# x is turned without its norm, the tokens' factors follow at the evacuations, and the value columns are the first products

## The chip, the cores and the metric

One NeuronCore of a Trainium2 chip runs the whole program. The metric is device microseconds of one execution, the median of the runs shown. Before: 913.82 us, median of three runs (913.37 to 915.99).

## The reference, cut to what matters

The program computes two transformer blocks over 256 tokens of width 1024. The change touches the beginning of the first block alone:

```python
def rmsnorm(x, g):
    xf = x.astype(jnp.float32)
    y = xf * lax.rsqrt(jnp.mean(xf * xf, axis=-1, keepdims=True) + EPS)
    return (y * g.astype(jnp.float32)).astype(x.dtype)

hn = rmsnorm(h, norm_mix_g[l])
proj = hn @ w_in[l]
fq, fk, fv, ff, gq, gf, gi, gg = jnp.split(proj, split_idx, axis=-1)
```

The factor rsqrt(...) is one number per token, g one number per column of x. A factor per token can be applied to x or to each row of the product x g @ w_in; the result is the same but for rounding. fq, fk, fv (512 columns each) and ff (8 columns, forget gates) go to an attention; gq, gf, gi, gg (512 each) to a gated recurrence in chunks (q, forget gate, input, output gate).

## The kernel before

Each product is made in three passes of TensorE: both operands are split into a high part (fp32r) and a low part (the rest), and `mm3` (L205) adds high x high, low x high and high x low into PSUM. `split_to` (L321) splits the tokens' side: ScalarE writes the high part (L328 with a factor per partition), VectorE the low one (L329). The tokens lie transposed in `XT` = (`xh`, `xl`): 8 blocks of 128 columns of x on the partitions, 256 tokens along the row.

The weights come in granules of 1 MB (`Granule`, L31), loaded on SP's queue by `feed` (L117) into three raw buffers and split in two halves each (`split_next`, L129): ScalarE casts the high part (L142), VectorE subtracts (L143). At most six split halves exist; `pump` (L153) splits one more half after each unit of products. A unit is 24 products over one half granule: `a_units` (L210) puts weight columns on the partitions of the result and 256 tokens along the row; `b_units` (L244) and `fv_units` (L887) put 128 tokens on the partitions and 512 (or 2 x 260) columns along the row. Their results take both buffers of the PSUM tags `mm` (and, for fv, both of `tp`).

`emit` (L181) runs through the list of units: the unit's products, what the units before have put off (`then`, L196), one `pump`, the evacuation from PSUM, and the pieces hung on that index in the table at L1040 (the recurrence's `levels`, `forget`, the attention's S, T, V, tables, memory rows). TensorE's order is this one, written out. Inside `start` (L628) every engine's own instructions keep their written order; elsewhere a planner orders all engines but TensorE, by readiness and program order, and may put later instructions into gaps.

`start` loads the gain, x in two token halves and the first granule; TensorE runs twelve products on the identity meanwhile. Squares (ScalarE and VectorE), the power -0.5 on GpSimd (L297), the scaling of x (L651, L653), 16 transposes (L669) and 8 splits follow, with the first granule's split in four pieces, whose low parts GpSimd subtracts (L149). The units then come in the order gf, gq, gg, fv with ff, fq and fk, gi. gf is evacuated by a sigmoid, gq and gg by SiLU on ScalarE straight from PSUM (L753, L767), fq by ScalarE (L272), fk by VectorE (L270), fv and ff half by half on both (L909 to L911). `forget` (L920) transposes ff and takes the logarithm of its sigmoid; the recurrence's levels are eight small f32 products each (L792, L812) with VectorE's decays (L801, L802) and masked copies.

## Time and profile before

| | us |
|---|---|
| median of 3 runs | 913.82 |
| the profiled execution | 914.16 |
| its span, first to last instruction | 912.3 |
| TensorE busy | 898.0 (98%) |
| VectorE busy | 588.4 (64%) |
| ScalarE busy | 488.8 (54%) |
| GpSimd busy | 130.0 (14%) |

The profile comes from one execution. TensorE's busy time is that of overlapping products, whose ends are modelled, so the distance between starts tells more than the busy share. A wait is put down to the instruction or transfer that came last.

### The profile page before, as it was taken

What the parts mean: (1) busy time and instruction counts of PE and PEld (TensorE: products, weight loads), DVE (VectorE), ACT (ScalarE), POOL (GpSimd) and SP (SyncE); (2) the same over time, 40 slices, a digit from 0 to 9 for tenths busy, and PEclk for the clock granted to TensorE, in tenths of its full rate; (3) what the DMA queues carried; (4) which work ended last, traced back from release to release, by engine and by line L of the source; (5) the groups of instructions that cost most, each with busy time, mean ns of one, the idle gap of its engine ahead of it and who ended that gap; (6) DMA issues with size and microseconds to landing.
All of it is one profiled execution on the core that took longest, in us unless ns stands there. A gap on an engine that the chain in (4) does not pass through costs nothing.

```text
span 912.3 us, 15217 instructions
## 1 busy us (share of the span) xinstructions
PE 898.0 (98%) x6213; PEld 823.9 (90%) x6213; DVE 588.4 (64%) x858; ACT 488.8 (54%) x743; POOL 130.0 (14%) x141
## 2 busy tenths in 40 slices
PE   8999999999999999999999999999999999999997
PEld 7999898898899999999898899999998789999995
DVE  5778775755575444555776455776756777766664
ACT  6745753555455444444654545667443676555552
POOL 3102220000002111111104000221211201101101
PEclk9999999999999999999999999999999999999999
DMA  8776544543555555555374555434555455555531
GB/s 271 256 253 186 185 155 164 198 153 114 167 193 192 195 190 193 189 185 185 131 250 135 183 179 185 139 131 133 200 185 185 161 185 183 188 201 193 166 135 47
DMA packets 117972, 162.39 MB, mean 178 GB/s; under 512 B 3647, under 2 KB 90509, under 8 KB 117901
## 3 DMA queue, kind: packets, MB, share of 16 engines
q1 hardware_dynamic: 117901, 161.41, 53.4%
q8 instruction: 49, 0.80, 0.3%
q14 instruction: 22, 0.18, 0.1%
HBM read 160.34 MB, written 1.06 MB: 177 GB/s over the span
## 4 chain that ended last, share of the span: by engine, by line
PE 90%; DVE 4%; ACT 2%; DMA 2%; POOL 1%; issue 1%; SPq 0%; DVEq 0%; POOLq 0%; ACTq 0%
PE mm L206 19%; PE mm L207 19%; PE mm L208 19%; PE s L208 8%; PE s L206 8%; PE s L207 8%; DMA w<-in_w_in_dram 2%; PE s L792 1%; POOL sm L297 1%; DVE wl L143 1%; PE tp L1068 1%; PE s L1060 1%; PE tp L337 1%; ACT wh L142 1%; PE s L1212 1%
## 5 line engine op out<-in xcount | busy, mean ns | idle before, releaser
L143 DVE TENSOR_TENSOR wl<-w,wh 128x1024 fp32r<-128x1024 f32 (+1 forms) x283 | 355.4, 1261 | 182.4 <-ACT wh L142 180.8
L142 ACT CAST wh<-w 128x1024 fp32r<-128x1024 f32 (+1 forms) x284 | 296.1, 1048 | 306.0 <-PE mm L207 190.2
L206 PE MATMUL mm<-xh,wh 128*128 128x256 f32 x1120 | 317.8, 284 | 0.0
L207 PE MATMUL mm<-xl,wh 128*128 128x256 f32 x1120 | 313.9, 280 | 0.3
L208 PE MATMUL mm<-xh,wl 128*128 128x256 f32 x1120 | 313.3, 280 | 0.0
L206 PEld LDWEIGHTS mm<-xh,wh 128*128 128x128 f32 x1120 | 211.3, 189 | 3.9 <-issue 2.3
L207 PEld LDWEIGHTS mm<-xl,wh 128*128 128x128 f32 x1120 | 211.2, 189 | 2.0 <-DVE xl L329 0.7
L208 PEld LDWEIGHTS mm<-xh,wl 128*128 128x128 f32 x1120 | 211.3, 189 | 0.0
L206 PE MATMUL s<-wh,mh 128*128 128x512 f32 x176 | 69.8, 396 | 0.0
L207 PE MATMUL s<-wl,mh 128*128 128x512 f32 x176 | 69.0, 392 | 0.0
L208 PE MATMUL s<-wh,ml 128*128 128x512 f32 x168 | 66.1, 393 | 0.0
L297 POOL TENSOR_TENSOR sm<-sm,half 128x1 f32<-128x1 f32 (+2 forms) x24 | 20.3, 847 | 234.2 <-DVE sm L310 221.7
L1103 POOL TENSOR_TENSOR r<-r 128x512 f32<-128x512 f32 x16 | 25.3, 1583 | 148.6 <-ACT r L1101 148.6
L206 PE MATMUL mm<-eh,wh 128*128 128x256 f32 x160 | 45.7, 286 | 0.0
L207 PE MATMUL mm<-el,wh 128*128 128x256 f32 x160 | 44.8, 280 | 0.0
L208 PE MATMUL mm<-eh,wl 128*128 128x256 f32 x160 | 44.7, 280 | 0.0
L208 PE MATMUL s<-wh,mh 128*128 128x512 f32 x112 | 44.1, 393 | 0.0
L1362 POOL TENSOR_TENSOR r<-r 128x512 f32<-128x512 f32 x11 | 21.4, 1946 | 148.0 <-DVE r L1350 124.2
L206 PE MATMUL s<-wh,ml 128*128 128x512 f32 x104 | 40.9, 394 | 0.0
L207 PE MATMUL s<-wl,ml 128*128 128x512 f32 x104 | 40.7, 392 | 0.0
L207 PEld LDWEIGHTS s<-wl,mh 128*128 128x128 f32 x176 | 33.1, 188 | 6.9
L206 PEld LDWEIGHTS s<-wh,mh 128*128 128x128 f32 x176 | 33.1, 188 | 6.7
(273 smaller groups left out, 1377.7 us busy)
## 6 DMA issues: line engine op xcount, KB each, us to landing
w<-in_w_in_dram SPq DMA_DIRECT2D x39, 1024.0 KB
w<-in_w_dram SPq DMA_DIRECT2D x32, 1024.0 KB
w<-in_w_up_dram SPq DMA_DIRECT2D x22, 1024.0 KB
w<-in_w_down_dram SPq DMA_DIRECT2D x11, 1024.0 KB
w<-in_w_xkv_dram SPq DMA_DIRECT2D x8, 1024.0 KB
w<-in_w_out_dram SPq DMA_DIRECT2D x8, 1024.0 KB
w<-in_w_xq_dram SPq DMA_DIRECT2D x4, 1024.0 KB
w<-in_w_xo_dram SPq DMA_DIRECT2D x4, 1024.0 KB
```

The costliest lines, as they stand in the source:

```text
L142: S.copy(hi, src)
L143: low.tensor_tensor(lo, src, hi.bitcast(F32), op=ALU.subtract)
L206: PE.matmul(o, lh, rh, start=first, stop=False)
L207: PE.matmul(o, lh, rl, start=False, stop=False)
L208: PE.matmul(o, ll, rh, start=False, stop=last)
L297: G.tensor_tensor(r[:, :n], v[:, :n], half.to_broadcast([P, n]), op=ALU.pow)
L337: PE.transpose(o[:, k * P:(k + 1) * P], xn[:, kk * P:(kk + 1) * P], ident)
L792: PE.matmul(o, k_[:, x], q2, start=True, stop=True)
L1060: PE.matmul(s[:, t, :], xq[:, j, t * P:(t + 1) * P], xkT[:, j, :], start=(c == 0), stop=(c == 1))
L1068: PE.matmul(o[:, c * T:(c + 1) * T], xv[:, m, cs], pt[:, m, :], start=(m == 0), stop=(m == 1))
L1103: G.tensor_tensor(tt, ra, ra, op=ALU.mult)
L1362: G.tensor_tensor(yv, yg, yv, op=ALU.mult)
```

## The change

- The first granule is now the upper half (512 rows) of the 520 columns of fv and ff, loaded in three transfers between the two halves of x; the gain vector is loaded on ScalarE's queue. Eight products on the identity stand in for twelve.
- x is transposed as it is, one token half after the other; the splits are of 128x128 with the gain as factor. After each half come the twelve products of the first half granule with these tokens (`fv_part`). All low pieces of the first granule are subtracted by VectorE.
- The squares, sums and powers come behind that; the tokens' factors go to `rt` (a column per token half) and, by one product of ones with a diagonal, to `rB` (the 256 factors in a row on every partition; `row_factors`).
- Evacuations multiply by the tokens' factor: `ev_token` and `ev_gf` on VectorE with `rB`, SiLU and sigmoid in place afterwards on ScalarE; gg, fv, ff and gi with `rt` on ScalarE or VectorE.
- The units come in the order fv (the other three), gf, gq, gg, fq and fk, gi; the table of pieces is adapted: `forget` at index 4, the levels at 12 to 20.

```diff
...
@@ -142,11 +138,11 @@
             S.copy(hi, src)
             low.tensor_tensor(lo, src, hi.bitcast(F32), op=ALU.subtract)
         else:
-            k = g.nk // 2
+            k = shape[1] // 2
             for p in (np.s_[:, 0:k, :], np.s_[:, k:, :]):
                 def piece(p=p):
                     S.copy(hi[p], src[p])
-                    G.tensor_tensor(lo[p], src[p], hi[p].bitcast(F32), op=ALU.subtract)
+                    V.tensor_tensor(lo[p], src[p], hi[p].bitcast(F32), op=ALU.subtract)
                 pieces.append(piece)
         feed()
 
@@ -202,10 +198,13 @@
         later.append(go)
 
 
-    def mm3(o, lh, ll, rh, rl, first, last):
+    def mm3(o, lh, ll, rh, rl, first, last, rl_last=False):
         PE.matmul(o, lh, rh, start=first, stop=False)
-        PE.matmul(o, lh, rl, start=False, stop=False)
-        PE.matmul(o, ll, rh, start=False, stop=last)
+        if rl_last:
+            PE.matmul(o, ll, rh, start=False, stop=False)
+        PE.matmul(o, lh, rl, start=False, stop=last and rl_last)
+        if not rl_last:
+            PE.matmul(o, ll, rh, start=False, stop=last)
 
     def a_units(src, xt, evac, nk=8):
 
@@ -624,13 +623,24 @@
     hgrn_g = vt[:, 100:101]
     subln_g = vt[:, 101:102]
     w_in = a["w_in"][0]
+    rt = const.tile([P, 2], F32, name="rt")
+    rB = R[3][:, 1792:2048]
+    rB2 = rB.unsqueeze(1).to_broadcast([P, 2, T])
 
     def start():
         xin = a["x"][0].rearrange("(t p) d -> p t d", p=P)
         grow = R[5][0:8, 0:P]
-        nc.sync.dma_start(grow, a["norm_mix_g"][0].rearrange("(k p) -> k p", p=P))
-        for t in range(2):
-            nc.sync.dma_start(h[:, t, :], xin[:, t, :])
+        nc.scalar.dma_start(grow, a["norm_mix_g"][0].rearrange("(k p) -> k p", p=P))
+
+        w0 = stream[0]
+        w0.raw = wraw.tile([P, w0.nk, w0.ncol], F32, tag="w", name=nm("w"))
+        src = w0.src.rearrange("(k p) c -> p k c", p=P)
+        nc.sync.dma_start(h[:, 0, :], xin[:, 0, :])
+        for k in range(2):
+            nc.sync.dma_start(w0.raw[:, k, :], src[:, k, :])
+        nc.sync.dma_start(h[:, 1, :], xin[:, 1, :])
+        nc.sync.dma_start(w0.raw[:, 2:4, :], src[:, 2:4, :])
+        at_dma[0] = 1
         feed()
         V.memset(half, -0.5)
         V.memset(one, 1.0)
@@ -638,35 +648,34 @@
         g = const.tile([P, 8], F32, name="g8")
 
         o = mm_t()[:, 0:P]
-        for _ in range(12):
+        for _ in range(8):
             PE.matmul(o, ident, ident, start=True, stop=True)
         go = mm_t()[:, 0:8]
         PE.transpose(go, grow, ident[0:8, 0:8])
-        o = [x.rearrange("p (k t) -> p k t", k=2) for x in (s_t(), s_t(), s_t(), s_t(), tp_t(), tp_t())]
-        o = [o[k][:, 0, :] for k in range(6)] + [o[k][:, 1, :] for k in (2, 3)]
-
-        def scale(t, n, r):
-            x = xn_half(t)[:, HALVES[n]]
-            if n > t:
-                S.mul(x, h[:, t, HALVES[n]], r[:, 0:1])
-            else:
-                V.tensor_scalar(x, h[:, t, HALVES[n]], r[:, 0:1], None, op0=ALU.mult)
-
+        V.tensor_copy(g, go)
+        pieces = []
+        for _ in range(2):
+            split_next(pieces)
+
+        def turn(t):
+
+            o = [s_t(), s_t()]
+            for k in range(8):
+                PE.transpose(o[k // 4][:, k % 4 * P:(k % 4 + 1) * P], h[:, t, k * P:(k + 1) * P], ident)
+            for k in range(8):
+                split_to(XT, np.s_[:, k, t * P:(t + 1) * P], o[k // 4][:, k % 4 * P:(k % 4 + 1) * P], g[:, k:k + 1])
+                if k % 2 and len(pieces) > 2 * (1 - t):
+                    pieces.pop(0)()
+
+        for t in range(2):
+            turn(t)
+            fv_part(0, t)
+        release()
         ss = [sm_t(), sm_t()]
-        for n in range(2):
-            square(h[:, 0, HALVES[n]], ss[0][:, n:n + 1], (S, V)[n])
-        r0 = rstd_row(ss[0])
-        scale(0, 0, r0)
-        for n in range(2):
-            square(h[:, 1, HALVES[n]], ss[1][:, n:n + 1], (S, V)[n])
-        scale(0, 1, r0)
-        r1 = rstd_row(ss[1])
-        for n in range(2):
-            scale(1, n, r1)
-        V.tensor_copy(g, go)
         for t in range(2):
-            for k in range(8):
-                PE.transpose(o[k][:, t * P:(t + 1) * P], xn_half(t)[:, k * P:(k + 1) * P], ident)
+            for n in range(2):
+                square(h[:, t, HALVES[n]], ss[t][:, n:n + 1], (S, V)[n])
+            V.tensor_copy(rt[:, t:t + 1], rstd_row(ss[t])[:, 0:1])
 
         st1 = ppool.tile([P, 768], F32, tag="P", name="st1")
         st2 = ppool.tile([P, 768], F32, tag="P", name="st2")
@@ -678,16 +687,6 @@
         nc.sync.dma_start(st1[101:102, :P], a["subln_g_2"])
         nc.sync.dma_start(st2[0:88, :P], a["conv_w_2"][0, 0:2].rearrange("l (c p) -> (l c) p", p=P))
         lvlf = ppool.tile([P, 768], F32, tag="PT", name="lvlf")
-        pieces = []
-        for _ in range(2):
-            split_next(pieces)
-        for p in pieces[0:2]:
-            p()
-        for k in range(8):
-            split_to(XT, np.s_[:, k, :], o[k], g[:, k:k + 1])
-            if k in (5, 7):
-                pieces[k // 2]()
-
         def vectors():
             pv = tp_t()
             PE.transpose(pv[:, 0:102], st1[0:102, :P], ident[0:102, 0:102])
...
+        def row_factors():
+
+            ones, diag = R[4][:, 0:P], R[4][:, P:3 * P]
+            G.memset(ones, 1.0)
+            for t in range(2):
+                V.tensor_scalar(diag[:, t * P:(t + 1) * P], ident, rt[:, t:t + 1], None, op0=ALU.mult)
+            o = s_t()[:, 0:T]
+            PE.matmul(o, ones, diag, start=True, stop=True)
+            V.tensor_copy(rB, o)
+
         def load_tables():
             nc.sync.dma_start(lvlf[:, 0:512], a["c_lvl"])
             nc.sync.dma_start(fbias, a["fox_f_bias"].rearrange("o h -> h o"))
@@ -729,12 +738,13 @@
             V.tensor_scalar(nlam, nlam, -0.2, None, op0=ALU.add)
 
         start.vectors, start.tables, start.difference = vectors, tables, difference
-        start.load_tables, start.load_later = load_tables, load_later
+        start.load_tables, start.load_later, start.row_factors = load_tables, load_later, row_factors
 
     def start_in_order():
         with tc.manual_schedule():
             start()
 
+    stream.append(Granule(w_in[0:512, 1024:1544], 4, 520, False))
     do(start_in_order)
 
 
@@ -750,7 +760,9 @@
     def ev_gf(g):
         def ev(i, o):
             s = slice(g * 512, (g + 1) * 512)
-            S.activation(f_[:, s], o, AF.Sigmoid)
+            V.tensor_tensor(f_[:, s].rearrange("p (b t) -> p b t", b=2), o.rearrange("p (b t) -> p b t", b=2), rB2,
+                            op=ALU.mult)
+            S.activation(f_[:, s], f_[:, s], AF.Sigmoid)
 
             def rest():
                 for b in range(2):
@@ -762,9 +774,16 @@
             then(rest)
         return ev
 
-    def ev_silu(dst):
+    def ev_token(dst, scale=None, silu=False):
+
         def ev(i, o):
-            S.activation(dst, o, AF.Silu)
+            d, o = (x.rearrange("p (b t) -> p b t", b=2) for x in (dst, o))
+            if scale is None:
+                V.tensor_tensor(d, o, rB2, op=ALU.mult)
+            else:
+                V.scalar_tensor_tensor(d, o, scale, rB2, op0=ALU.mult, op1=ALU.mult)
+            if silu:
+                S.activation(dst, dst, AF.Silu)
         return ev
 
 
@@ -884,34 +903,37 @@
 
     ff = []
 
-    def fv_units():
-        gs_ = [Granule(w_in[kq * 512:(kq + 1) * 512, 1024:1544], 4, 520, False) for kq in range(2)]
-        st = {}
-
-        def unit(i):
-            if i == 0:
-                st["o"] = [(mm_t(), tp_t()) for _ in range(2)]
-            w = part(gs_[i // 2], i % 2)
+    fv_g = [stream[0], Granule(w_in[512:D, 1024:1544], 4, 520, False)]
+    fv_o = []
+
+    def fv_part(i, t):
+        if len(fv_o) == t:
+            fv_o.append((mm_t(), tp_t()))
+        w = part(fv_g[i // 2], i % 2)
+        tok = slice(t * P, (t + 1) * P)
+        for k in range(2):
+            for c in range(2):
+                cs = slice(c * 260, (c + 1) * 260)
+
+                mm3(fv_o[t][c][:, 0:260], r32(xh[:, 2 * i + k, tok]), r32(xl[:, 2 * i + k, tok]),
+                    w[0][:, k, cs], w[1][:, k, cs], i == 0 and k == 0, i == 3 and k == 1, True)
+
+    def fv_unit(i):
+        for t in range(2):
+            fv_part(i, t)
+        release()
+
+        def ev():
             for t in range(2):
-                tok = slice(t * P, (t + 1) * P)
-                for k in range(2):
-                    for c in range(2):
-                        cs = slice(c * 260, (c + 1) * 260)
-                        mm3(st["o"][t][c][:, 0:260], r32(xh[:, 2 * i + k, tok]), r32(xl[:, 2 * i + k, tok]),
-                            w[0][:, k, cs], w[1][:, k, cs], i == 0 and k == 0, i == 3 and k == 1)
-            release()
-
-            def ev():
-                for t in range(2):
-                    copy = V.tensor_copy if t else S.copy
-                    o = st["o"][t]
-                    ff.append(sm_t())
-                    copy(fv[:, t, 0:260], o[0][:, 0:260])
-                    copy(ff[t], o[1][:, 252:260])
-                    copy(fv[:, t, 260:512], o[1][:, 0:252])
-            return ev if i == 3 else None
-
-        return [(lambda i=i: unit(i), gs_[i // 2] if i % 2 == 0 else None) for i in range(4)]
+                o, r = fv_o[t], rt[:, t:t + 1]
+                ff.append(sm_t())
+                for dst, src in ((fv[:, t, 0:260], o[0][:, 0:260]), (ff[t], o[1][:, 252:260]),
+                                 (fv[:, t, 260:512], o[1][:, 0:252])):
+                    if t:
+                        V.tensor_scalar(dst, src, r, None, op0=ALU.mult)
+                    else:
+                        S.mul(dst, src, r)
+        return ev if i == 3 else None
 
 
     fox_bias = [x.rearrange("p (e c) -> p e c", e=2) for x in
@@ -1025,27 +1047,30 @@
 
 
     m_load, m_s0, m_s1, m_t0, m_t1 = mem_rows("mem", "norm_mem_g", R[5], s_t)
-    u_ = []
+    u_ = [(lambda i=i: fv_unit(i), fv_g[1] if i == 2 else None) for i in range(1, 4)]
     for g in range(2):
         u_ += a_units(cols(w_in, 2056, g), XT, ev_gf(g))
     for g in range(2):
-        u_ += a_units(cols(w_in, 1544, g), XT, ev_silu(q_[:, g * 512:(g + 1) * 512]))
-    u_ += b_units(w_in[:, 3080:3592], XT, lambda t, o: ev_silu(gs[:, t * 512:(t + 1) * 512])(0, o))
-    u_ += fv_units()
+        u_ += a_units(cols(w_in, 1544, g), XT, ev_token(q_[:, g * 512:(g + 1) * 512], silu=True))
+    u_ += b_units(w_in[:, 3080:3592], XT, lambda t, o: S.activation(gs[:, t * 512:(t + 1) * 512], o, AF.Silu,
+                                                                    scale=rt[:, t:t + 1]))
     for g in range(2):
-        u_ += a_units(cols(w_in, 0, g), XT, ev_to(R[2][:, g * 512:(g + 1) * 512], 0.125))
-        u_ += a_units(cols(w_in, 512, g), XT, ev_to(R[2][:, 1024 + g * 512:1024 + (g + 1) * 512]))
-    u_ += rows(w_in, 2568, 1, gi) + grid(xkw, 0, 4, R[5], None, ME)
+        u_ += a_units(cols(w_in, 0, g), XT, ev_token(R[2][:, g * 512:(g + 1) * 512], 0.125))
+        u_ += a_units(cols(w_in, 512, g), XT, ev_token(R[2][:, 1024 + g * 512:1024 + (g + 1) * 512]))
+    u_ += b_units(w_in[:, 2568:3080], XT, lambda t, o: (V.tensor_scalar(gi[:, 1, :], o, rt[:, 1:2], None, op0=ALU.mult)
+                                                        if t else S.mul(gi[:, 0, :], o, rt[:, 0:1])))
+    u_ += grid(xkw, 0, 4, R[5], None, ME)
     fox = Heads(fox_scores, fox_turn, fox_pv)
-    run(u_, {
-        1: [lambda: start.vectors()], 2: [lambda: start.load_tables()], 6: [lambda: start.tables()],
-        7: [lambda: start.load_later()], 9: [levels[0]], 11: [levels[1]],
-        12: [m_load, levels[2], lambda: start.difference()], 13: [levels[3]], 14: [levels[4]], 15: [forget],
-        16: [levels[5], m_s0], 17: [levels[6]], 18: [levels[7], m_s1, load_bias(0)], 19: [levels[8]],
-        20: [load_bias(1, 2, 3)], 21: [fox.S(0)], 23: [fox.T(0), fox.S(1)], 25: [fox.V(0), m_t0],
-        26: [fox.S(2), m_t1], 27: [fox.T(1)], 28: [fox.S(3), h_out(0)], 29: [fox.V(1), h_out(1)],
+    at = {
+        2: [lambda: start.load_tables()], 3: [lambda: start.row_factors()], 4: [lambda: start.vectors()], 5: [forget],
+        8: [load_bias(0)], 7: [lambda: start.tables()], 11: [lambda: start.load_later()],
+        13: [levels[0], m_load], 14: [levels[1]], 15: [levels[2], lambda: start.difference()], 16: [levels[3], m_s0],
+        17: [levels[4]], 18: [levels[5], m_s1], 19: [levels[6]], 20: [levels[7]], 21: [levels[8], fox.S(0)],
+        22: [load_bias(1, 2, 3)], 23: [fox.T(0)], 24: [fox.S(1)], 25: [fox.V(0), m_t0],
+        26: [fox.T(1), m_t1], 27: [fox.S(2)], 28: [fox.V(1), h_out(0)], 29: [fox.S(3), h_out(1)],
         30: [fox.T(2)], 31: [h_turn(0)], 32: [fox.V(2), fox.T(3)], 33: [h_turn(1)], 34: [fox.V(3)],
-    })
+    }
+    run(u_, {i - 1: x for i, x in at.items()})
     fill_xv = rows(xkw, D, 2, xv, ME)
     out_stage(a["w_out"][0], MT, Tail, lambda: [gain("norm_x_g")], fill_xv[0:4])
 
```

## Rows read from the trace of the kernel before

**Rows 1.** The profile's page: busy time by engine; the chain that ended last.
```profile
PE 898.0 (98%) x6213; PEld 823.9 (90%) x6213; DVE 588.4 (64%) x858; ACT 488.8 (54%) x743; POOL 130.0 (14%) x141
...
PE 90%; DVE 4%; ACT 2%; DMA 2%; POOL 1%; issue 1%; SPq 0%; DVEq 0%; POOLq 0%; ACTq 0%
```
**Rows 2.** Windows: stretch, length, busy time per engine, granted clock, DMA share, GB/s.
```profile
0.00:5.00 5.00, 3.65 (x17) 3.66 (x18) 0.22 (x3) 1.41 (x2) 0.69 (x6) 1.00 0.49 169
5.00:10.00 5.00, 3.84 (x22) 2.93 (x21) 3.42 (x9) 3.07 (x7) 2.39 (x3) 1.00 1.10 320
10.00:15.00 5.00, 4.11 (x27) 3.50 (x28) 3.96 (x10) 4.27 (x11) 3.96 (x5) 1.00 1.09 347
...
14.83:35.00 20.17, 20.17 (x174) 20.17 (x173) 16.40 (x27) 17.61 (x19) 5.07 (x6) 1.00 0.77 252
35.00:146.00 111.00, 109.80 (x854) 101.20 (x854) 80.94 (x147) 58.12 (x102) 16.83 (x22) 1.00 0.60 197
```
**Rows 3.** Timeline of TensorE, the start: start us, us, engine, line, operation.
```profile
1.34 5.49 PE L642 MATMUL mm<-ident 128*128 128x128 f32 x24 [1.34 <-POOL ident masks.py:199]
...
7.12 0.66 PE L669 MATMUL s<-ident,r 128*128 128x128 f32 x4
...
11.26 0.38 PE L206 MATMUL mm<-xh,wh 128*128 128x256 f32 x1
...
15.23 0.28 PE L206 MATMUL mm<-xh,wh 128*128 128x256 f32 x1
...
18.07 0.25 PE L693 MATMUL tp<-ident,st 102*128 102x102 f32 x1
```
**Rows 4.** Timeline of the other engines and SP's queue, the start.
```profile
1.18 0.83 SPq L633 DMA_DIRECT2D h<-in_x_dram  x2
...
4.87 0.63 ACT L304 ACTIVATE junk<-h 128x512 bf16<-128x512 f32 x1 [2.87 <-DMA h<-in_x_dram]
...
5.98 0.56 POOL L297 TENSOR_TENSOR sm<-sm,half 128x1 f32<-128x1 f32 x1 [4.69 <-DVE sm L310]
...
10.73 1.57 ACT L328 ACTIVATE xh<-s,g 128x256 fp32r<-128x256 f32 x4 [1.55 <-DVE g L666]
...
11.24 1.66 DVE L329 SCALAR_TENSOR_TENSOR xl<-s,g,xh 128x256 fp32r<-128x256 f32 x4 [0.60 <-ACT xh L328]
...
11.63 0.95 POOL L710 MEMSET r<- 128x1024 f32 x1
...
13.62 2.55 POOL L149 TENSOR_TENSOR wl<-w,wh 128x512 fp32r<-128x512 f32 x2 [1.04 <-ACT wh L148]
```
**Rows 5.** Groups by line and shape: count | busy us, mean ns | idle before.
```profile
L143 DVE TENSOR_TENSOR wl<-w,wh 128x1024 fp32r<-128x1024 f32 x36 | 45.6, 1277 | 10.8 <-ACT wh L142 10.8
...
L357 DVE CUSTOM_DVE_ANT_0 P<-s,r 128x128 f32<-128x128 f32 x8 | 2.3, 288 | 5.2 <-issue 3.6 <-DMA r<-negF 1.6
...
L142 ACT CAST wh<-w 128x1024 fp32r<-128x1024 f32 x36 | 37.1, 1052 | 47.7 <-PE mm L207 23.5 <-PE tp L208 8.2 <-issue 7.2
...
L909 ACT COPY r<-mm 128x260 f32<-128x260 f32 x1 | 0.4, 376 | 1.8 <-PE mm L208 1.8
...
L812 PE MATMUL s<-r,r 128*128 128x128 f32 x16 | 1.9, 275 | 0.0
```
**Rows 6.** Timeline around the two stalls behind the start: TensorE, ScalarE, VectorE.
```profile
36.35 0.39 PE L208 MATMUL mm<-wh,xl 128*128 128x512 f32 x1
36.88 0.50 PE L206 MATMUL mm<-wh,xh 128*128 128x512 f32 x1
...
67.14 0.27 PE L924 MATMUL s<-ident,sm 128*8 128x128 f32 x1
67.90 0.27 PE L924 MATMUL s<-ident,sm 128*8 128x128 f32 x1 [0.49 <-DVE sm L910]
...
36.24 0.59 ACT L767 ACTIVATE r<-mm 128x512 f32<-128x512 f32 x1
...
66.22 1.21 DVE L143 TENSOR_TENSOR wl<-w,wh 128x1024 fp32r<-128x1024 f32 x1
```

More of the change, by code (lines that the diff above doesn't have):

```diff
@@ L121, in feed @@
             src = g.src.rearrange("(k p) c -> p k c", p=P)
-            if at_dma[0]:
-                nc.sync.dma_start(g.raw, src)
-            else:
-                for c in (slice(0, P), slice(P, 2 * P)):
-                    nc.sync.dma_start(g.raw[:, :, c], src[:, :, c])
+            nc.sync.dma_start(g.raw, src)
             at_dma[0] += 1
@@ L644, in start @@
         PE.transpose(go, grow, ident[0:8, 0:8])
-        o = [x.rearrange("p (k t) -> p k t", k=2) for x in (s_t(), s_t(), s_t(), s_t(), tp_t(), tp_t())]
-        o = [o[k][:, 0, :] for k in range(6)] + [o[k][:, 1, :] for k in (2, 3)]
-        def scale(t, n, r):
-            x = xn_half(t)[:, HALVES[n]]
-            if n > t:
-                S.mul(x, h[:, t, HALVES[n]], r[:, 0:1])
-            else:
-                V.tensor_scalar(x, h[:, t, HALVES[n]], r[:, 0:1], None, op0=ALU.mult)
-        ss = [sm_t(), sm_t()]
-        for n in range(2):
-            square(h[:, 0, HALVES[n]], ss[0][:, n:n + 1], (S, V)[n])
-        r0 = rstd_row(ss[0])
-        scale(0, 0, r0)
-        for n in range(2):
-            square(h[:, 1, HALVES[n]], ss[1][:, n:n + 1], (S, V)[n])
-        scale(0, 1, r0)
-        r1 = rstd_row(ss[1])
-        for n in range(2):
-            scale(1, n, r1)
-        V.tensor_copy(g, go)
+        V.tensor_copy(g, go)
[14 more added lines that the diff above has]
+        release()
+        ss = [sm_t(), sm_t()]
         for t in range(2):
-            for k in range(8):
-                PE.transpose(o[k][:, t * P:(t + 1) * P], xn_half(t)[:, k * P:(k + 1) * P], ident)
+            for n in range(2):
+                square(h[:, t, HALVES[n]], ss[t][:, n:n + 1], (S, V)[n])
+            V.tensor_copy(rt[:, t:t + 1], rstd_row(ss[t])[:, 0:1])
         st1 = ppool.tile([P, 768], F32, tag="P", name="st1")
```

## The prediction

> **What bounds the kernel now.** I read the page's busy times and its chain of waits first. TensorE is busy for 98% of the span and holds 90% of the chain that ended last [rows 1], so only two kinds of edit can move the time: fewer TensorE passes, or fewer holes between them. Next the table by stretch shows where the holes lie [rows 2]: from 15 to 35 us TensorE has none, in the 111 us after that 1.2 us, and the change touches nothing behind that. The large hole is the start. TensorE's own timeline tells its size [rows 3]: the first product of the projection is issued at 11.26, the stream runs evenly from 15.23 (24 products done), and 24 more take until 18.07, 0.118 us each. At that pace the first 24 would have begun at 15.23 - 2.84 = 12.39 us. I call this the virtual start; whatever moves it moves the end by as much, as long as nothing starves later. The other engines' timeline says what it is made of [rows 4]: x lands at 4.87, then come squares, the power on GpSimd, a scaling, transposes, splits, one behind the other. The stalls inside the stretch are two [rows 6]: 36.35 to 36.88 (a PSUM bank that ScalarE's SiLU frees late) and 67.14 to 67.90 (forget-gate columns whose copy waits behind a 1.21 us subtraction on VectorE).
>
> **The start after the change.** The norm leaves the chain; what stands on it is x, transposes, splits, weights. All times here are estimates from the rows.
>
> x's first half landed 3.69 us after its issue at 1.18; it is now the first issue on SP's queue (0.72), so 4.4. The gain vector goes by ScalarE's queue, which waits for x anyway. Eight warm-up products instead of twelve take 5.49 x 8/12 = 3.7 us and end at 5.0. [...]
>
> Bytes: 0.85 MB are in by 5 us, 2.45 by 10, then 0.35 per us [rows 2]. A landing is seen some 0.7 behind its byte (x's 0.52 MB: some 0.8 before the 0.85 at 5, at about 0.4 per us, so 4.2, seen at 4.87), and all comes 0.46 earlier. So the two first slices of weights are there at 5.1 and 5.9, x's other half at 7.5, the remaining slices at 9.2, the second granule at 12.4.
>
> Splits: sixteen of 128x128 replace eight of 128x256. The trace has no such split; above stands the 256-column one (1.57/4 = 0.39 on ScalarE, 1.66/4 = 0.42 on VectorE [rows 4]), below half of it. I take 0.28 on both, near the 288 ns of the other 128x128 operation that reads PSUM on VectorE [rows 5]. A weight piece of 520 columns: 0.6 on VectorE (half of L143) and no more on ScalarE (half of L142 is 0.5). The low pieces come from GpSimd, where two took 2.55, onto VectorE, which becomes the queue that sets the pace: 16 x 0.28 + 4 x 0.6 = 6.9 us.
>
> Half 0: ScalarE begins at 6.1, VectorE at 6.5, the second low piece is done at 9.0. The twelve products wait for it and end at 9.6; then TensorE turns half 1 (bank done 10.2), VectorE goes on at 10.6 and is through at 14.2. The twelve products of half 1 end at 12.3 and the next 24 at 15.2, with every operand there in time. That would be a virtual start of 15.2 - 48 x 0.12 = 9.5.
>
> It isn't kept. The squares, freed from the chain, now stand in the queues behind the splits and ahead of the second granule. ScalarE: last split 13.5, two squares of 0.63 with their read-outs, the cast (1.05) done at 15.9. VectorE: square and sum (1.1, from x's landing at 4.87 to GpSimd's start at 5.98 [rows 4]) until 15.2, then the factor's copy waits for GpSimd's power (0.56 and the handing over) until 15.9, a second square until 16.8, and the granule's subtraction (1.14 apart) done between 17.1 and 17.9, as it lands ahead of the second square or behind it. I take 17.5: 22 of the unit's 24 products are behind it and end at 20.1, the virtual start is 20.1 - 72 x 0.12 = 11.5. **Term 1: 11.5 - 12.4 = -0.9 us**, with ends -2.9 (subtraction ahead of all squares) and +0.9 (behind both factor copies and the diagonals: done 19.3, virtual start 13.3).
>
> **The other terms.** Row factors: one f32 product over 256 columns, twice an L812 product (1.9 us for eight, two records each [rows 5]), **+0.45** on TensorE. Ones and diagonals are ready before, on engines with idle time.
>
> Value columns first: the bank of gf's first unit now waits for fv's evacuation of token half 0 on ScalarE (0.38 as L909 [rows 5], and the handing over), with only the 0.45 product as cover: **+0.3**; a cast in front makes it 1.3. Behind this multiply stand two small ones on ScalarE; the next casts are five parts ahead.
>
> Forget gate: its transposes come two units after the values' evacuation, so the 0.76 gap [rows 6] goes but for a normal 0.1: **-0.65**. Its exponential and logarithm come into a ScalarE that is 87% busy from 15 to 35 us [rows 2]; PSUM no longer hangs on ScalarE there, and gates and q are freed by VectorE. What is late next is the levels, which moved behind gs; each still has a unit's products as cover.
>
> Evacuation: gf, q and fq now pass VectorE with the tokens' factor, as fk did; six more of 512 columns, some 0.65 each (half of L143). gf's sigmoid and q's SiLU follow in place, off TensorE's path. q to gs keeps its stall: before, SiLU behind a cast cost 0.53 less a normal 0.12 [rows 6]; now a VectorE product behind a subtraction of 1.2: **+0.1** (between -0.3 and +0.8). VectorE is 81% busy from 15 to 35 us and 73% in the 111 after [rows 2]; 3.9 us over both leave it below TensorE's pace, with the levels' small products as cover where they come: 0 (up to +1).
>
> SP's queue: the fourth granule's load waits for the first's buffer, free at 13 (before 16.2, the end of GpSimd's last piece [rows 4]); the small vector loads may stand behind it, but TensorE wants them only at some 24.
>
> Sum -0.9 + 0.45 + 0.3 - 0.65 + 0.1 = -0.7 us. The profiled execution took 914.16 (span 912.3), so 913.5; it stands 0.34 above the median of 913.82, which makes **913.1**.
>
> **Rivals.**
> A (0.50) is this sum: 913.1, its own range 911.8 to 914.8.
> B (0.22): the planner, which fills idle time with whatever is ready, puts the second granule's cast and subtraction ahead of the squares. For it: both engines wait for TensorE's turn of half 1, and a memset of a much later unit stood between GpSimd's pieces before (11.63 [rows 4]). Against it: the granule lands at 12.4, when the squares are ready and older. Virtual start 9.5, the sum -2.7: 911.1.
> C (0.16): the other side. VectorE takes both factor copies, with their two waits for GpSimd, ahead of the subtraction: virtual start 13.3, and a cast ahead of the values' evacuation: +0.9 + 0.45 + 1.3 - 0.65 + 0.1 = +2.1: 915.9. With A's other terms it turns to slower where that subtraction ends after 18.2. For it: the start has its order written out. Against it: the planner may use each wait of 0.6.
> [...]
> [...]
>
> **Chances.** 0.3%, 2.7 us, is about what a measurement can tell from no change. Faster than 911.1: two thirds of B and a little of A, 0.22. Slower than 916.5: part of C, or C with D, 0.12. Between: 0.66. The range reaches to B's further end and past C: 910.3 to 916.3.
>
> **What would show it.** Right: the first product near 7.2, 48 products done near 15.2, then a gap of some 2 us at the second granule's first half with VectorE at squares and factor copies; no gap at the forget gate; one of under half a us at gf's start. Wrong: the third unit's products following without a gap (B), a gap past 18.2 (C), product spacing of 0.24 beyond 7 us (D), or new gaps among the levels, which would mean that VectorE is the bound there.

## The result, and the profile after

The changed kernel takes **947.7 us** (median of 4 runs, 946.7 to 948.1) against 914.1 (median of four runs of the kernel before): slower by a ratio of 1.036 [1.034, 1.038]. The forecast of 913.1 was wrong, sign and size.

Counting the projections' products along TensorE's timeline says where the 33.6 us between the two profiled executions (914.16 and 947.77) were lost. The k-th product is issued at (us):

| product | before | after | behind by |
|---|---|---|---|
| 48th | 17.95 | 27.92 | 10.0 |
| 96th | 23.82 | 33.65 | 9.8 |
| 120th | 26.66 | 43.70 | 17.0 |
| 744th | 143.58 | 168.88 | 25.3 |
| 5448th (near the end) | 894.20 | 927.73 | 33.5 |

So there are three losses: the start, some places up to 169 us, and a steady 8.2 us over all that follows, where not one instruction differs (the instructions of all four engines behind the 744th product are the same, in the same order). The windows of after, in the columns of [rows 2]:

```profile
10.00:15.00 5.00, 1.44 (x6) 0.90 (x4) 0.00 (x0) 0.85 (x3) 0.00 (x0) 0.50 1.07 369
14.83:35.00 20.17, 15.72 (x96) 14.92 (x96) 15.27 (x35) 11.69 (x25) 1.49 (x4) 0.72 0.62 205
35.00:146.00 111.00, 102.90 (x741) 94.62 (x742) 77.35 (x140) 54.57 (x88) 14.32 (x20) 0.94 0.52 166
```

From 10 to 15 us VectorE does nothing at all, in the stretch that was to be its busiest, and TensorE does 6 records. The granted clock is 0.50, where [rows 2] had 1.00. TensorE's timeline has the holes one by one, to be read beside [rows 3] and [rows 6]:

```profile
11.02 0.42 PE L204 MATMUL mm<-wh,xl 128*128 128x260 f32 x1
17.51 0.58 PE L205 MATMUL mm<-wl,xh 128*128 128x260 f32 x1 [6.07 <-DVE wl L145]
...
33.65 0.28 PE L205 MATMUL tp<-wl,xh 128*128 128x260 f32 x1
38.02 1.22 PE L718 MATMUL s<-r 128*128 128x256 f32 x2 [4.09 <-DVE r L716]
...
65.42 0.39 PE L207 MATMUL mm<-wh,xl 128*128 128x512 f32 x1
67.38 0.51 PE L202 MATMUL mm<-wh,xh 128*128 128x512 f32 x1 [1.57 <-DVE r L782]
...
115.72 0.28 PE L207 MATMUL mm<-xh,wl 128*128 128x256 f32 x1
119.51 0.90 PE L345 MATMUL tp<-ident,P 128*128 128x128 f32 x3 [3.50 <-POOL P L993]
```

A releaser named here only says who came last; the cause is what that engine itself waited for. For the first two holes, in the timelines of VectorE, SP's queue and ScalarE:

```profile
15.66 0.43 DVE L707 CAST lvl<-lvlf 128x512 uint8<-128x512 f32 x1 [5.99 <-DMA lvlf<-in_c_lvl_dram]
...
37.69 0.28 DVE L716 TENSOR_SCALAR r<-ident,rt 128x128 f32<-128x128 f32 x1
```
```profile
4.13 4.36 SPq L722 DMA_DIRECT2D lvlf<-in_c_lvl_dram  x1
...
25.80 0.38 SPq L122 DMA_DIRECT2D w<-in_w_in_dram  x1
```
```profile
5.72 1.28 ACT L327 ACT_TABLE_LOAD   x1 [5.72 <-DVE g L655]
...
7.80 0.37 ACT L327 ACTIVATE xh<-s,g 128x128 fp32r<-128x128 f32 x1 [0.42 <-DVE xl L328]
...
32.37 1.05 ACT L138 CAST wh<-w 128x1024 fp32r<-128x1024 f32 x1 [2.52 <-DMA w<-in_w_in_dram]
33.32 0.62 ACT L303 ACTIVATE junk<-h 128x512 bf16<-128x512 f32 x1
```

VectorE stands 6 us in the middle of half 0's splits, before a cast of the level table that is first read at 72.8 us; the planner drew it forward, and the table's load lies behind two granules. The second square of half 1 (33.32) stands behind a cast of the fourth granule, whose load was issued at 25.80 only. So the second row factor, and the diagonal made of it (37.69), come at 38. ScalarE's first split begins at 7.01, behind a table load that the gain released at 5.72; in the kernel before, this load was over long before x came:

```profile
0.71 1.28 ACT L304 ACT_TABLE_LOAD   x1 [0.71 <-PEq L1423]
```

The hole at 115.7 is a norm on GpSimd (L993) behind masks (L973) that wait for the bias loads:

```profile
117.81 1.29 POOL L973 TENSOR_TENSOR r<-r,causal 128x256 f32<-128x256 f32 x2 [1.22 <-DMA r<-negF]
119.08 0.72 POOL L993 TENSOR_SCALAR P<-P,sm 128x128 f32<-128x128 f32 x2
```

The steady loss shows in the groups by shape, 230 to 880 us (count | busy, mean ns). Before:

```profile
L207 PE MATMUL mm<-xl,wh 128*128 128x256 f32 x903 | 252.6, 280 | 0.0
L207 PE MATMUL s<-wl,mh 128*128 128x512 f32 x126 | 49.3, 392 | 0.0
```

After:

```profile
L205 PE MATMUL mm<-xl,wh 128*128 128x256 f32 x857 | 241.6, 282 | 0.0
L205 PE MATMUL s<-wl,mh 128*128 128x512 f32 x128 | 50.7, 396 | 0.0
```

2 to 4 ns on every product, with the clock at 1.00.

### The profile page after: what moved, and what is told of

Its sections match the earlier page's. It is cut to its first block, busy times and chain, and to the rows that moved or that the text cites. A ratio compares the mean times of both kernels' runs of the same rounds, so it can differ in the third digit from the quotient of the medians.

```text
span 946.0 us, 15234 instructions
## 1 busy us (share of the span) xinstructions
PE 916.9 (97%) x6207; PEld 838.2 (89%) x6207; DVE 595.5 (63%) x878; ACT 486.3 (51%) x745; POOL 123.5 (13%) x138
## 4 chain that ended last, share of the span: by engine, by line
PE 89%; DMA 3%; DVE 3%; ACT 2%; issue 1%; POOL 1%; SPq 0%; DVEq 0%; ACTq 0%; POOLq 0%
PE mm L202 19%; PE mm L205 19%; PE mm L207 19%; PE s L205 8%; PE s L207 8%; PE s L202 8%; DMA w<-in_w_in_dram 2%; PE s L811 1%; DVE wl L139 1%; PE tp L336 1%; DMA lamv<-in_lambda_k_dram 1%; DMA w<-in_w_xkv_dram 1%; POOL sm L296 1%; PE tp L1093 1%; PE s L1085 1%
## 5 line engine op out<-in xcount | busy, mean ns | idle before, releaser
L1128 POOL TENSOR_TENSOR r<-r 128x512 f32<-128x512 f32 x16 | 25.3, 1583 | 151.2 <-ACT r L1126 151.2
L202 PE MATMUL mm<-wh,xh 128*128 128x512 f32 (+1 forms) x96 | 39.7, 414 | 4.8 <-ACT wh L144 2.1
L205 PE MATMUL mm<-wl,xh 128*128 128x512 f32 (+1 forms) x96 | 38.2, 398 | 6.3 <-DVE wl L145 6.3
```

Of the source, the lines that this page charges most:

```text
L202: PE.matmul(o, lh, rh, start=first, stop=False)
L205: PE.matmul(o, lh, rl, start=False, stop=last and rl_last)
L1128: G.tensor_tensor(tt, ra, ra, op=ALU.mult)
```

## The experiments

Theory: the loss is the sum of separate causes, none of them the moved norm as such: queue order at the start, a late row factor, GpSimd's norm at fox, and a 32-byte shift of the matrix buffers by the new tile `rt`. The rivals stand in each expectation. "Before" ran again beside each group, at 914.5 to 915.4.

**The slow pace.** The changed kernel with its factors in a tile that is there anyway:

```
-    lam = const.tile([P, 4], F32, name="lam")
+    lam = const.tile([P, 8], F32, name="lam")
...
-    rt = const.tile([P, 2], F32, name="rt")
+    rt = lam[:, 4:6]
```


> The changed kernel, with the two row factors put into spare columns of a tile that was there already, so that the matrix buffers lie again at the offsets that they had in the kernel before (129856, 154816 and 179776 instead of 32 bytes more). Nothing else differs. Theory (the offset slows each product of the whole rest): the mean spacing of products of 256 columns goes back from 118.5 to about 116.7 ns, and the 8.2 us that the changed kernel loses between 146 us and its end are gone: about 939.5 us. Rival (the slow pace comes from the order that the planner chose later, not from the offset): 947 us, within 1 us of the changed kernel.

937.2 us, 10.5 less than the changed kernel. From the 744th to the 5448th product it takes 749.7 us (after 758.9, before 750.6). The theory holds; its row for the second form above:

```profile
L205 PE MATMUL s<-wl,mh 128*128 128x512 f32 x128 | 50.2, 392 | 0.0
```

The same from the other side, the kernel before with 32 idle bytes (8 in use), `rt = const.tile([P, 2], F32)`, set to zero by VectorE and read by nobody:

> The kernel before, with an added constant tile of 32 bytes (one memset writes it, nobody reads it), so that the matrix buffers lie 32 bytes further. Theory (the offset slows each product): the products' spacing rises by 1.1 to 1.5% everywhere, 914 + 9.5 = about 923.5 us, with no one stage that loses it. Rival (the pace is the later order's): 914 us, within 0.5 us.

924.9 us, ratio 1.0110 [1.0086, 1.0133]. The loss grows evenly, 9.2 us at the 5448th product, from 0.2 ahead at the 48th. With 64 bytes (`[P, 16]`):

> The kernel before, with the same idle constant tile made 64 bytes wide: the matrix buffers lie 64 bytes further and are again multiples of 64. Theory (it is the half step of 32 bytes that costs, not the place): the time of before, within 1 us of it. Rival (any shift from the place of before costs, by a relation between two buffers or a place in a larger block): 919 to 924 us.

917.5 us, 1.0027 [1.0016, 1.0039], between the two expectations. The trace parts them: 2.6 us are lost before the 24th product and 0.8 in the 880 us behind, so the pace is that of before. And 32 bytes behind the raw granules (a pool of its own, ahead of the split parts' pool):

> The kernel before, with 32 idle bytes between the buffers of raw granules and those of their two split parts: the raw granules stay where they were, the split parts (and what lies behind them) move by 32 bytes. Theory (TensorE reads the split parts as the moving side of its products, and that reading is slower from a place that is no multiple of 64): all of the loss, 923 to 925 us. Rival (the loss is in the loads that write the raw granules, or in the engines that read them): the time of before, within 1 us.

926.5 us, 1.0124 [1.0106, 1.0142]; 3.4 us at the start, 9.1 behind it. The product of the same form in these kernels (shifted by 32, by 64, and the parts alone by 32):

```profile
L207 PE MATMUL s<-wl,mh 128*128 128x512 f32 x128 | 50.7, 396 | 0.0
```
```profile
L207 PE MATMUL s<-wl,mh 128*128 128x512 f32 x128 | 50.2, 393 | 0.0
```
```profile
L208 PE MATMUL s<-wl,mh 128*128 128x512 f32 x128 | 50.7, 396 | 0.0
```

The raw granules' place doesn't matter (9.1 us lost behind the start with the parts alone moved, 9.2 at the 5448th product with both). A split part that lies 32 bytes off its place of before (154816 or 179776 by the first of these expectations, multiples of 64) costs 2 to 4 ns a product, as moving operand (512 columns) and as stationary one (256; the tokens' side lies ahead of the parts and didn't move). The tiles allocated behind the parts moved with them, so that they have no share is argued, not shown.

**The start.** The tables' loads are made to follow the row factor (a tiny copy into each tile first):

```
+        G.tensor_copy(dist[:, 0:1], rt[:, 1:2])
+        G.tensor_copy(lamv[:, :, 0:1], rt[:, 1:2].unsqueeze(1).to_broadcast([P, 4, 1]))
...
         lvlf = ppool.tile([P, 768], F32, tag="PT", name="lvlf")
+        G.tensor_copy(lvlf[:, 0:1], rt[:, 1:2])
```


> The changed kernel, with the loads of the level table, the distances and the lambda vectors made to follow the row factors (each tile first gets a tiny copy of the factor from GpSimd), so that the planner cannot put their loads and VectorE's casts of them among the first splits. Theory (VectorE's queue stood for 6 us behind the cast of a table whose load lay behind two granules): the first product comes at 11.5 to 12 us instead of 17.5, and the start loses 6 to 10 us less: about 940 us (937 to 942). Rival (the start is late because of the two engines' turns at one bank and the clock, and the cast only stood in a gap that was there anyway): 946 to 948 us.

939.9 us, 7.8 less; the 96th product comes at 26.16 instead of 33.65, with 3.4 us at half the clock ahead of it instead of 17.1. The wait for the factor stays and is even longer:

```profile
31.54 0.80 PE L721 MATMUL s<-r 128*128 128x256 f32 x1 [5.10 <-DVE r L719]
```

Instead, the squares ahead of each turn (the factor's last steps stay behind it, unlike what the expectation says):

```
-        for t in range(2):
-            turn(t)
-            fv_part(0, t)
-        release()
         ss = [sm_t(), sm_t()]
         for t in range(2):
             for n in range(2):
                 square(h[:, t, HALVES[n]], ss[t][:, n:n + 1], (S, V)[n])
+            turn(t)
+            fv_part(0, t)
             V.tensor_copy(rt[:, t:t + 1], rstd_row(ss[t])[:, 0:1])
+        release()
```


> The changed kernel, with the squares of each half and its factor ahead of that half's turn, so that the factors cannot stand behind the fourth granule's cast on ScalarE. Theory (the stop of 4.9 us at 33 to 38 us is the wait for the second half's factor, and the clock's fall behind it costs about 2 us more): that stop is gone, about 941 us (939 to 943), unless the squares push the first splits later by their own 1.5 to 2.5 us, which would leave 942 to 943.5. Rival (the stop is anyway the wait for the fourth granule, whose load is issued at 25.8 us): about 947 us, and the gap at 34 to 38 us stands in the trace with another releaser.

940.1 us, 7.6 less. The 96th product is where it was (33.57), the 120th 6.8 us earlier (36.87): the stop and the half clock behind it are gone.

What is the clock's own share? Dummy products in the two waits of the start:

```
+            for _ in range((10, 28)[k] if (i, t) == (0, 0) else 0):
+                PE.matmul(fv_o[1][0][:, 0:P], ident, ident, start=True, stop=True)
```


> The changed kernel, with 10 products of the identity ahead of the first product and 28 ahead of the second block (their results are overwritten), in the two waits of the start, so that TensorE is busy while it waits. Every wait stays as it was. Theory (the clock is halved from 9.2 to 26.3 us because TensorE stood; about 33 products and a turn then take twice their time): granted clock 1.0 to 25 us, the 96th product 3 to 4 us earlier, 943.5 to 945 us. Rival (behind the wait the splits set the pace, not the clock): clock up, but within 1 us of 947.7; or the clock stays at half although TensorE is busy: 947 to 950 us.

944.6 us, 3.1 less and within the theory's range, but not where I expected it. The 96th product comes 1.8 us later, not 3 to 4 earlier. The windows of this kernel:

```profile
9.00:23.00 14.00, 10.74 (x87) 9.88 (x86) 5.54 (x17) 3.96 (x12) 0.80 (x2) 1.00 0.79 277
23.00:30.00 7.00, 6.43 (x30) 5.96 (x29) 6.75 (x11) 6.17 (x12) 0.00 (x0) 0.51 0.69 231
...
35.00:45.00 10.00, 7.64 (x63) 7.34 (x62) 7.44 (x16) 4.55 (x8) 1.01 (x2) 1.00 0.97 318
```

Dummy work does hold the clock (1.00 from 9 to 23 us); the fall comes behind the next wait without it (2.6 us at 18.8 to 21.4). Up to the 96th product nothing is won; the win is behind the stop for the factor, which in the changed kernel runs at half the clock (its row 38.02: two products take 1.22 us). Here no dummy product stands in that stop, but it is 2.35 us long instead of 4.09, as the 96th product is late, and the clock stays full:

```profile
38.11 0.70 PE L718 MATMUL s<-r 128*128 128x256 f32 x2 [2.35 <-DVE r L716]
```

**Fox.** The first pair's norm on VectorE alone (`eng = V if i or p == 0 else G`):

> The changed kernel, with the first fox pair's weights normed by VectorE alone instead of half by GpSimd. Theory (GpSimd's norm stands behind three pairs of masks that wait for loads; TensorE stops 3.5 us for it at 116 us, and runs at half clock for 7 us behind): 942 to 943 us, and no low clock at 118 to 125 us. Rival (the stop is filled by what VectorE takes over, or another wait stands right behind): 946 to 948 us.

941.3 us, 6.4 less. The window 110 to 146 us, after and here: the stop and the low clock are gone together.

```profile
110.00:146.00 36.00, 32.50 (x209) 27.62 (x208) 20.69 (x52) 19.06 (x42) 6.86 (x12) 0.91 0.45 138
```
```profile
110.00:146.00 36.00, 36.00 (x262) 31.29 (x261) 26.05 (x70) 22.40 (x52) 10.37 (x14) 1.00 0.52 169
```

**All together.** Offsets, tables, squares (here all four between the two turns), fox, and the far loads tied to the query columns, as here:

```
+            gate = R[0][:, 1024:1025]
+            G.tensor_copy(lamv[:, :, 0:1], gate.unsqueeze(1).to_broadcast([P, 4, 1]))
+            G.tensor_copy(cnt[:, 0, 0:1], gate)
+            G.tensor_copy(pw[:, 0, 0:1], gate)
             for i, n in enumerate(("lambda_q1_2", "lambda_q2_2", "lambda_k1_2", "lambda_k2_2")):
```


> The changed kernel with four repairs at once: the row factors in a tile that was there (offsets as before); the loads of the tables tied to the row factors, and those of the lambda vectors, counts, pool weights and memory rows to the query columns; all four squares between the two turns; the weights of the first fox pair normed by VectorE alone. Theory (the causes found are separate and add up): 947.7 - 10.5 (offset, measured) - 7.8 (tables, measured) - 7.6 (squares, measured) - 5 (fox stop 3.5 and the low clock behind it) = 917, range 914 to 920. Rival (the repairs of the start overlap, as the turns at one bank and the fourth granule's load hold the start anyway): 922 to 926.

921.4 us, 1.0078 [1.0051, 1.0105]: 26.3 of the 33.6 are back. The four alone sum to 10.5 + 7.8 + 7.6 + 6.4 = 32.3, so they overlap by 6 (the squares stand elsewhere here, too), near the rival's number: the start has other limits behind the first. One, by the row at 7.80, is the PSUM bank that ScalarE and VectorE share:

```
-                PE.transpose(o[k // 4][:, k % 4 * P:(k % 4 + 1) * P], h[:, t, k * P:(k + 1) * P], ident)
+                PE.transpose(o[k % 2][:, k // 2 * P:(k // 2 + 1) * P], h[:, t, k * P:(k + 1) * P], ident)
...
```


> The kernel with the four repairs, and neighbouring slices of a turn in two PSUM banks in place of four in one. Theory (ScalarE's split of a slice waits 0.42 us for VectorE's read of the same bank, so a slice costs 0.79 us instead of about 0.35 to 0.5): the splits of a half are done 1.5 to 3 us earlier, 2 to 3 us less than the kernel with the four repairs, and no 0.42 us idle times behind VectorE on ScalarE's line of splits. Rival (the casts of the weights, put between the splits, take that room anyway): within 1 us of the kernel with the four repairs.

921.4 us (918.6 to 923.8), nothing by the median. By the trace the mechanism is right: the 0.42 us waits are gone (two splits in 0.62),

```profile
7.15 0.62 ACT L329 ACTIVATE xh<-s,g 128x128 fp32r<-128x128 f32 x2 [0.15 <-PE s L666]
```

the clock is 1.00 up to 45 us, and the 96th product comes at 23.02, 4.5 us earlier and **0.8 ahead of the kernel before**. Its profiled execution is 3.3 us shorter than that without banks (span 916.9 against 920.2), but it was the fastest of its four, and the medians don't bear it out. Part of the 4.5 us is the clock's: without banks the profiled execution ran at half the clock from 9.2 to 19.4 us, here it did so nowhere before 52. Behind the 96th product stands the second factor again, now behind VectorE's remaining splits:

```profile
24.62 0.70 PE L724 MATMUL s<-r 128*128 128x256 f32 x2 [1.31 <-DVE r L722]
```

Why two readers of one bank take turns is not shown; 0.42 us of idle time is what it costs a split here. Next, the factor's last steps moved up:

```
+        for t in range(2):
+            G.tensor_copy(rt[:, t:t + 1], rstd_row(ss[t])[:, 0:1])
         turn(1)
         fv_part(0, 1)
-        for t in range(2):
-            V.tensor_copy(rt[:, t:t + 1], rstd_row(ss[t])[:, 0:1])
```


> The kernel with all repairs and the banks, and the factor's last steps (sum, power, copy) right behind the squares, the copy on GpSimd, so that VectorE's splits of the second half don't stand ahead of them. Theory (TensorE's stop of 1.6 us at 23.0 to 24.6 us is the wait for the second factor): no stop behind the 96th product, 1.3 to 1.9 us off, 919.5 to 920 against 921.4. Rival (the next granule's cast ends there as well, its load is issued at 15.4 us and landed at 21 us): less than 0.7 us.

**916.6 us**, 1.0016 [1.0002, 1.0029] of before. By the medians the gain of 4.8 is more than expected, but no trace shows it: this profiled execution was the slowest of its ten (918.7), and its span of 916.8 is that of the kernel before it. In it the stop didn't vanish but changed its owner: the value columns' way out on ScalarE, behind a cast.

```profile
24.70 0.59 PE L724 MATMUL s<-r 128*128 128x256 f32 x2
27.32 0.39 PE L204 MATMUL mm<-xh,wh 128*128 128x256 f32 x1 [2.02 <-ACT r L945]
```

Two attempts on what is left. Query columns copied out of PSUM by ScalarE, the factor on the copy:

```
+            if scale is None and silu:
+                S.copy(d, o)
+                V.tensor_tensor(d, d, rB2, op=ALU.mult)
```


> The same, and the query columns leave PSUM by a copy on ScalarE, the factor follows on the copy in VectorE's own time. Theory (TensorE's stop of 2.7 us at 49.4 us is a PSUM bank that VectorE frees late, since the factor's product has to pass VectorE's queue of 1.2 us subtractions; behind it the clock is half for 3.4 us): the stop and the low clock are gone, 3 to 4 us off, 916 to 917, and the 744th product within 1 us of the kernel before's 143.6 us. Rival (ScalarE's extra copies push its casts of the weights, or the stop comes one unit later): less than 1 us.

917.9 us, no gain. The stop of 2.7 us was read in the kernel ahead of the early factors; with them it isn't there (no two starts of TensorE at q lie over 0.6 us apart), so the edit had nothing to remove. The next stop, before the levels, grew from 1.8 to 3.3. And the first granule cast wholly in the first turn:

```
-                if k % 2 and len(pieces) > 2 * (1 - t):
+                if k % 2 and pieces:
```


> The kernel with early factors, with all four pieces of the first granule cast in the first turn, so that its buffer is free and the fourth granule's load issued some 2 to 3 us earlier (at 15.4 us until now). Theory (the stop of 2.6 us at 24.7 us is the wait for that granule's casts, and the low clock behind it comes with it): the stop is under 0.7 us, 2 to 3.5 us off, 913 to 914.5. Rival (the pieces push the second turn's splits by their 1.3 us, and the products behind wait for VectorE in any case): within 1 us of 916.6, or slower.

925.2 us, slower, for a reason neither side named: the planner drew a cast and a subtraction of the *second* granule among the splits. ScalarE waits there for the granule's load, and VectorE for the cast, as it did for the level table; the fourth granule's load came no earlier (15.47 us):

```profile
11.98 1.06 ACT L140 CAST wh<-w 128x1040 fp32r<-128x1040 f32 x1 [1.71 <-DMA w<-in_w_in_dram]
...
13.07 1.24 DVE L141 TENSOR_TENSOR wl<-w,wh 128x1040 fp32r<-128x1040 f32 x1 [1.98 <-ACT wh L140]
```

**The start of before.** What the 64-byte shift lost at the start (2.6 us), in the timelines of VectorE and GpSimd of that kernel:

```profile
8.75 3.85 DVE L655 TENSOR_SCALAR r<-h,sm 128x512 f32<-128x512 f32 x2 [0.67 <-POOL sm L297]
```
```profile
8.76 2.67 POOL L149 TENSOR_TENSOR wl<-w,wh 128x512 fp32r<-128x512 f32 x2
```

In the kernel before:

```profile
8.67 1.90 DVE L653 TENSOR_SCALAR r<-h,sm 128x512 f32<-128x512 f32 x2 [0.67 <-POOL sm L297]
```
```profile
8.74 2.96 POOL L149 TENSOR_TENSOR wl<-w,wh 128x512 fp32r<-128x512 f32 x2
```

VectorE begins 70 ns ahead of GpSimd there and 10 ns ahead in the shifted kernel (40 ns, and 3.88 us, with the parts alone shifted). The granted clock of the shifted kernel is 0.50 from 10 to 15 us as well, against 1.00 in [rows 2]. If so small a difference decides, taking VectorE's part away should narrow the spread:

```
-            if n > t:
+            if n > t or t:
                 S.mul(x, h[:, t, HALVES[n]], r[:, 0:1])
```


> The kernel before, with both halves of the second token block scaled by ScalarE (one of them was VectorE's), so that VectorE has no such instruction at 8.7 us, when GpSimd's first subtractions begin. Theory (VectorE's scaling and GpSimd's subtraction exclude each other, and which comes first by some ns decides over 2 us and over the clock behind): no VectorE instruction over 0.7 us before 10 us, and the times lie within 1.5 us of each other, at 913.0 to 914.5, without the upper half of before's spread. Rival (the spread has another origin; ScalarE's extra 0.5 us is simply added): the same spread, 914.5 to 915.5.

913.9 us (913.2 to 915.1, 10 runs) beside 914.5 (913.1 to 916.8, 13 runs), ratio 0.9993 [0.9983, 1.0004]: the spread is 2.0 us instead of 3.7, not the 1.5 expected, and the medians can't be told apart. In the kernel before, VectorE's scaling of this shape took 0.49 us at 6.58, 0.49 at 8.67 (70 ns ahead of GpSimd's first subtraction) and 1.49 at 9.1, in the middle of it; the subtractions took 1.54 and 1.45 us there and 1.29 at 13.62. That the two engines exclude each other is my estimate from these times, and no run shows it; by the starts VectorE was ahead in all three kernels and took 1.90, 3.85 and 3.88 us, so a lead in the profile doesn't tell who runs on undisturbed. That the meeting makes the spread of before is not shown: the profiled execution without it, at 915.1 the slowest of its ten, has its 24th product 1.6 us later than before's (16.72 against 15.11), with TensorE at half the clock:

```profile
10.00:15.00 5.00, 4.72 (x21) 4.04 (x20) 3.31 (x8) 5.00 (x13) 4.42 (x4) 0.50 1.09 347
```

## Why the prediction was wrong

**Term 1 (-0.9 us, measured +9.8 at the 96th product).** The step that failed is the order of the queues: "it isn't kept" let only the squares and the factor copies come between splits and granule. The planner also drew forward whatever the later units had issued, casts that wait for loads among them, and in a queue worked off in order one such wait holds everything (VectorE's 5.99 us before the level table's cast). I used a memset drawn forward [rows 4] as evidence for rival B and didn't ask what else could be. With such work tied away and two banks, the 96th product came 0.8 us ahead of before in one execution, the fastest of four (0.8 behind with the early factors). That this is the -0.9 of the sum is luck: the route was another, with the squares between the turns and the 48th product at 17.31 instead of 15.2.

**Splits at 0.28 us** took 0.37 on ScalarE and came 0.79 apart (7.01, 7.80, 8.58), as four slices shared a bank; in before, neighbours lay in different ones. They were to begin at 6.1, a time that no run shows: the eight transposes ran from 5.36 for 1.30 us, and the first split began at 7.01, behind a table load of 1.28 us that had no term.

**SP's queue.** I had the fourth granule's load issued at 13 and only small loads near it; it came at 25.8, when a buffer was free at last, and the second factor behind its cast. "Row factors +0.45" had no price for being late; the product itself was near it (0.67 us, at half the clock), the distance of the starts before it was 4.4, and from the 96th to the 120th product 7.2 us were lost.

**The clock.** Rival D of the chances stood for half the clock from the first product on. In the changed kernel it came later: the first product is issued at 8.73, the granted clock is 1.00 up to 9.2 us, and the eight transposes behind the warm-up took 1.30 us, beside the 1.91 of the next eight at half the clock. It fell in or right behind TensorE's waits, three times (9.2 to 26.3 us first). Where the first wait was filled (the dummy products) or 1.01 us long instead of 2.07 (two banks), the first fall isn't there; at 1.75 us (all pieces early) it is. I had no term for what a new wait costs beyond itself.

**"The change touches nothing behind that"** (146 us) was wrong by 8.2 us: a tile of 32 bytes moved every matrix buffer. **Fox** (6.4) had no term either: I followed the levels and not the bias loads (the last five were issued at 108.6 to 110.6 us, before at 84.6 to 86.7).

**Right:** the forget gate's gap is gone; q to gs does wait for VectorE, but the distance of the starts grew from 0.53 to 1.96 us, by 1.43 instead of the 0.8 at most. With the causes found repaired, the change still costs 2.1 us (916.6 against 914.5, with an interval that just excludes no difference), where A had a gain of 0.7. So the moved norm as such has little part in the 33 us; that it gains anything is not shown.

Open: what holds the repaired kernel 2 us behind; the runs moved that stop and didn't remove it. Its profiled execution (918.7) loses 4.2 us from the 96th to the 120th product, at the stop of 2.02 us and 3.4 us of half clock behind it, and 1.8 up to the 744th.

## What to carry to other kernels

Where a planner fills idle time, an edit's cost isn't its own chain but what may now be drawn ahead of it: list what waits for a load among the work issued later, and tie it to something late. Check the byte offsets of matrix operands after adding any small tile (32 bytes cost 1.1% here). Price a new wait of TensorE by the stop and by the half clock behind it (here 4.09 us, and 7).

## What the runs showed of the hardware

- A product whose split operand lies 32 bytes off its place of before takes 282 instead of 280 ns (256 columns) or 396 instead of 392 (512): 1.1% of this kernel. With a shift of 64 bytes it is 393, and the pace is the old one.
- In the changed kernel TensorE's granted clock fell to 0.50 in or right behind waits of 2.07, 4.09 and 3.50 us, for 17, 7 and 7 us; it didn't behind one of 2.35 us in the kernel with dummy products. Products of the identity in a wait held it at 1.00 (9 to 23 us of that kernel).
- VectorE's two scalings beside GpSimd's subtractions took 3.85 us where they began 10 ns ahead of them, 3.88 at 40 ns, and 1.90 at 70 ns. One such scaling in the kernel before took 0.49 us at 6.58 and 1.49 at 9.1, beside a subtraction.
- ScalarE's first table load took 1.28 us in both kernels: from 0.71 us, while x was loaded, before; from 5.72, ahead of the first split, after.
